# Half 0's convolution split in two: two channel tiles before the recurrence's inverse, two after it

## The chip, the cores and the metric

One core of one Trainium2 chip runs the whole program in one launch. The metric is device time in microseconds (us); the time shown for a kernel is the median of its runs. The profile is of one further execution, and its time is given beside its span.

## The reference

One layer of a hybrid decoder over 1024 tokens of width 1024, with 256 memory tokens, all in float32. The input projection of the normed x has two uses: its first 1024 columns feed a causal convolution group of 512 channels, the others a recurrent (RWKV-7) group of 8 heads. What the change touches is this much of it:

```
h = rms_norm(x, g[0])
p = h @ w_in_first
y_conv = conformer_conv(p[..., :2 * D_CONV], ...)   # u * sigmoid(u'), 31 taps per channel, layer norm, silu
y_rwkv = rwkv7_mix(p[..., 2 * D_CONV:], ...)        # token-shift mix, gates, recurrence, group norm
x = x + rms_norm(concat(y_conv, y_rwkv) @ w_out, g[1])
mem_n = rms_norm(mem, mem_norm_g)
x = x + rms_norm(cross_attention(rms_norm(x, g[2]), mem_n, wq, wkv, wo), g[3])
x = x + rms_norm(swiglu(rms_norm(x, g[4]), w_gu, w_down), g[5])
```

## The kernel before

**Halves and phases.** The 1024 tokens are worked in two halves of TB = 512. For each half the kernel projects (`w_in_block`), prepares the recurrence's factors (`rwkv_prep`), inverts small triangular blocks (`rwkv_values`, `rwkv_inverse`), runs the recurrence over eight chunks of 64 tokens (`rwkv_chain`, whose results leave in `rwkv_out`), runs the convolution (`conv`), and then the output projection, cross-attention and feed-forward. Results of one phase go to DRAM tiles (pdr for mixer features, hd for the convolution's input, yd for the mixer's output) and are loaded from there by the next.

**Matmuls.** Every weight panel is split on chip in a high part (ScalarE, line 170) and a low part (VectorE, line 171), and each product is three matmuls (lines 193 to 195). One input panel of 128 features over 512 tokens is 24 matmuls of 512 columns. `wload` takes the raw panel in a ring of four tiles and the two parts in rings of two. All DMAs but a few go through SyncE's queue.

**The projection's columns.** `conv_cols` = (4, 0, 6, 2) and `mix_cols` = (20, 12, 8, 16, 14, 10, 18) name pairs of panels. Panel 20 carries the low-rank inputs, 12 and 14 the first and second two key tiles, 8 and 10 the receptance, 16 and 18 the values. A mixer panel is evacuated at lines 305 to 312, a convolution panel at lines 321 and 325. `rwkv_prep` is a generator: its first part works on head pairs 0 and 1 and needs the first keys; its second part begins with `norms(1)`, which needs both tiles of block 14. The last vector operation of a head pair is the gate product at line 549.

**The convolution.** Each of four channel tiles loads one row block `hin` from hd, starts its accumulator on ScalarE (line 348) and adds 30 taps on VectorE (line 350). When all four are done, `conv_norm` takes two sums over channels by matmul (lines 365 and 378), a reciprocal square root, and stores each tile to yd (line 392). The accumulators are one tile of four parts. The bias tile `cb` is one buffer that half 1's convolution takes over.

**The order.** The program is traced as one list, and a planner orders each engine's instructions from that list: an instruction that stands earlier goes first when its inputs and its tile are there. `weave` mixes two generators by the us that they say they cost; `fill` draws panels of half 1 into gaps of the output phases by the amounts in `self.fl`. The memory maps (`memory_maps`, lines 823 to 856) fold the attention's weights with the normed memory, four heads of them. Pools stand on two stacks, left and right, and a pool pushed after another was popped stands on its addresses and waits for its tiles one by one.

In before, half 0 goes: norm x and the memory; block 20; blocks 12, 8, 16; the preparation's first part; blocks 14, 10, 18; its second part; values, inverse; convolution panels; recurrence; and a weave of (two heads of maps, norm of half 1's x, two heads of maps, half 1's convolution panels, three of its mixer blocks) with the convolution of half 0. The last four mixer blocks are the filler of what follows. The pool conv0 stands on the left where the preparation and the inverse were.

Of the kernel before, what the change touches and what calls it, by code (L numbers as in the profile page):

```python
# [9 lines left out]
F32 = mybir.dt.float32  # L10
# [7 lines left out]
P = 128  # L18
# [3 lines left out]
TB = 512  # L22
NB = SEQ // TB
MEM = 256
DR = 512
# [36 lines left out]
def drain(*gens):  # L62
    for g in gens:
        for _ in g:
            pass


class Trunk:
# [259 lines left out]


    def conv(self, b, pool):  # L330
        acc = pool.tile([P, 4, TB], F32, tag="acc", name="acc")
        yield from self.conv_taps(b, pool, acc)
        yield from self.conv_norm(b, pool, acc)

    def conv_taps(self, b, pool, acc):
        nc = self.nc

        if b == 1:
            self.cb = self.cp.tile([P, 8], F32, tag="convb", name="convb")
            nc.scalar.copy(out=self.cb[:, 0:4], in_=self.col("conv_b"))  # L340
            nc.scalar.copy(out=self.cb[:, 4:8], in_=self.lbh)
        t0 = b * TB
        for j in range(4):
            h = pool.tile([P, 576], F32, tag="hin", bufs=2, name="hin")[:, 0:TB + CONVW - 1]
            nc.sync.dma_start(out=h, in_=self.hd[j * P:(j + 1) * P, t0:t0 + TB + CONVW - 1])
            a = acc[:, j, :]
            w = lambda k: self.cwh[:, j * CONVW + k:j * CONVW + k + 1]
            nc.scalar.activation(out=a, in_=h[:, 0:TB], func=AF.Identity, scale=w(0), bias=self.cb[:, j:j + 1])  # L348
            for k in range(1, CONVW):
                nc.vector.scalar_tensor_tensor(out=a, in0=h[:, k:k + TB], scalar=w(k), in1=a,  # L350
                                               op0=ALU.mult, op1=ALU.add)
                if k % 6 == 0:
                    yield 4.0

    def conv_norm(self, b, pool, acc):
# [2 lines left out]
        tmp = lambda name: pool.tile([P, TB], F32, tag="t", bufs=2, name=name)  # L358
        add = lambda out, x, y: nc.vector.tensor_tensor(out=out, in0=x, in1=y, op=ALU.add)
        sa, sb = tmp("lnsa"), tmp("lnsb")  # L360
        add(sa, acc[:, 0, :], acc[:, 1, :])
        add(sb, acc[:, 2, :], acc[:, 3, :])
        add(sa, sa, sb)
        ps = self.pn.tile([P, TB], F32, tag="n", name="psln")
        nc.tensor.matmul(ps, self.ones, sa, start=True, stop=True)
        for j in range(4):
            nc.vector.scalar_tensor_tensor(out=acc[:, j, :], in0=ps, scalar=-1.0 / DR, in1=acc[:, j, :],
                                           op0=ALU.mult, op1=ALU.add)
        yield 6.0
        sa = tmp("lnsq")  # L370
        nc.scalar.activation(out=sa, in_=acc[:, 0, :], func=AF.Square)
        for j in range(1, 4):
            sb = tmp("lnsq")
            nc.scalar.activation(out=sb, in_=acc[:, j, :], func=AF.Square)
            add(sb, sa, sb)
            sa = sb
        ps = self.pn.tile([P, TB], F32, tag="n", name="psln2")
# [4 lines left out]
        self.rsqrt(ry, rs, pool.tile([P, TB], F32, tag="t", bufs=2, name="lnt"))  # L382
        yield 6.0
        for j in range(4):
            a = acc[:, j, :]
            nc.vector.tensor_tensor(out=a, in0=a, in1=ry, op=ALU.mult)
            th = pool.tile([P, TB], F32, tag="t", bufs=2, name="lnth")
            sc, bi = self.lgh[:, j:j + 1], self.cb[:, 4 + j:5 + j]
            nc.scalar.activation(out=th, in_=a, func=AF.Tanh, scale=sc, bias=bi)
            nc.scalar.activation(out=a, in_=a, func=AF.Identity, scale=sc, bias=bi)  # L390
            nc.vector.scalar_tensor_tensor(out=a, in0=th, scalar=1.0, in1=a, op0=ALU.add, op1=ALU.mult)
            nc.sync.dma_start(out=self.yd[j * P:(j + 1) * P, t0:t0 + TB], in_=a)
            yield 2.0
# [550 lines left out]
    def run(self):  # L944
# [4 lines left out]
        def push(name, side):  # L949
            opened[name] = tc.tile_pool(name=name, bufs=1, side=side, reuse_waits="tile")  # L950
            return opened[name].__enter__()
# [3 lines left out]
                opened.pop(n).__exit__(None, None, None)  # L955


        self.fl = dict(res0=6.0, load0=6.0, soft0=5.0, res1=5.0, load1=16.0, soft1=0.0)
        self.filler = None
        self.credit = 0.0  # L960
        conv_cols, mix_cols = (4, 0, 6, 2), (20, 12, 8, 16, 14, 10, 18)
# [3 lines left out]

        a1 = push("a1", R)
        ev = push("ev", R)
        mk = push("mk", R)
        a0 = push("a0", R)
        h0, h1, mT = self.pairs(a0), self.pairs(a1), self.pairs(mk, MEM, "m")  # L970
        self.xn = 4
        self.xp = push("xa", L)
        self.normed(self.x, 0, (0, 4), h0, "g_mix", 2)
        drain(self.w_in_block(0, h0, ev, mix_cols[:1], 2))
        self.normed(self.mem, 0, (0, 2), mT, "g_mem", 2)
        pop("xa")
        self.lora_split(ev)
        self.nc.scalar.dma_start(out=self.hd[:, 0:CONVW - 1].rearrange("(j p) t -> p j t", p=P), in_=self.state[:, :, 0:CONVW - 1])
# [1 line left out]
        pp = push("prep0", L)  # L980
        prep = self.rwkv_prep(0, pp)
        next(prep)
        drain(self.w_in_block(0, h0, ev, mix_cols[4:]))
        drain(prep)
        pop("prep0")

        tp = push("tt0", L)
        TT = tp.tile([P, NCH * HP, CH], F32, tag="TT", name="TT")
        pp = push("inv0", L)
        self.rwkv_values(0, pp)  # L990
        self.rwkv_inverse(0, pp, TT)
        drain(self.w_in_block(0, h0, ev, conv_cols))
        pop("inv0", "a0")
        kv = push("kv", R)
        self.xn = 2
        self.xp = push("xb", R)
        kp = push("conv0", L)

        gp = push("gn0", L)
        mp = push("mix0", L)  # L1000
# [4 lines left out]
                yield 1.0 * 2  # L1005
        maps = self.memory_maps(mT, ev, kv)
        w1 = self.w_in_block(1, h1, ev, conv_cols)
        w1m = self.w_in_block(1, h1, ev, mix_cols[:3])
        main = chain(islice(maps, 16), next_norm(), maps, w1, w1m)
        drain(weave(main, self.conv(0, kp), 1.0))  # L1010
        pop("mix0", "gn0", "conv0", "tt0", "xb", "kv", "mk")
        self.filler = self.w_in_block(1, h1, ev, mix_cols[3:])

        yp = push("y0", L)
        a2 = push("a2", L)
# [106 lines left out]
```

## Time and profile before

| what | value |
|---|---|
| median of 3 runs | 1640.81 us (1639.69 to 1641.62) |
| profiled execution | 1639.56 us, span 1637.8 us |
| TensorE matmul busy | 1521.8 us (93%) |
| TensorE weight loads busy | 1240.5 us (76%) |
| VectorE busy | 1066.9 us (65%) |
| ScalarE busy | 685.9 us (42%) |
| mean granted TensorE clock | 0.967 |

Busy time is the time in which an engine executes; shares are of the span. Times in rows are us from the span's start. The matmuls' ends are modelled, so the spacing of their starts tells more than their length. L350 is line 350 of the kernel; PE is TensorE, PEld its weight loads, DVE VectorE, ACT ScalarE, SPq SyncE's queue.

### The profile page before, as it was taken

To read this page: it belongs to the slowest core of one execution; us is meant where nothing else is said; L and a number is where in the kernel's file an instruction comes from. 1 tells how busy PE (TensorE), PEld (TensorE's weight loads), DVE (VectorE), ACT (ScalarE), POOL (GpSimd) and SP (SyncE) were. 2 spreads that over 40 slices of the span, in tenths; PEclk is the share of its full clock that TensorE was granted. 3 is DMA by queue.
4 is the path that set the end of the run, shared out by engine and by line. 5 is a ranking of instruction groups with operands and counts; after the bars stand their busy time and mean duration, and the time that the engine had idled before them with its cause. 6 is when DMAs were issued, how large, how long until landed. Compare 5 with 4: busy or idle time off the path is not lost.

```text
span 1637.8 us, 22612 instructions
## 1 busy us (share of the span) xinstructions
PE 1521.8 (93%) x8688; PEld 1240.5 (76%) x8688; DVE 1066.9 (65%) x1704; ACT 685.9 (42%) x1064; POOL 54.6 (3%) x102
## 2 busy tenths in 40 slices
PE   7999878999659789699999999999999999999997
PEld 6787767877447577577788777888887888888886
DVE  5687675999879996686775455637537634344445
ACT  5645355544343336456323344524435332222222
POOL 1000100000000100100000000001001100000000
PEclk9999988999879899899999999999999999999999
DMA  6576995774344423545885444445236633333331
GB/s 201 176 230 183 297 339 153 258 234 142 103 141 158 143 86 93 190 124 150 234 248 139 143 145 138 149 124 200 87 97 225 231 98 95 101 92 101 92 90 52
DMA packets 175643, 257.36 MB, mean 157 GB/s; under 512 B 68912, under 2 KB 110000, under 8 KB 175536
## 3 DMA queue, kind: packets, MB, share of 16 engines
q1 hardware_dynamic: 174576, 255.08, 50.0%
q8 instruction: 68, 1.11, 0.3%
q10 hardware_dynamic: 960, 0.85, 0.2%
q14 instruction: 39, 0.32, 0.1%
HBM read 196.58 MB, written 59.31 MB: 156 GB/s over the span
## 4 chain that ended last, share of the span: by engine, by line
PE 85%; DVE 5%; DMA 4%; ACT 4%; issue 1%; SPq 0%; POOL 0%; DVEq 0%; POOLq 0%; ACTq 0%
PE psf L193 15%; PE psf L195 15%; PE psf L194 15%; PE pst L193 10%; PE pst L194 10%; PE pst L195 10%; PE psg L522 2%; DVE acc L350 1%; PE pstr L273 1%; PE pspr L436 1%; DVE wlo L171 1%; ACT whi L170 1%; DMA xt<-in_x_dram 1%; DVE ya L762 1%; PE psq L684 1%
## 5 line engine op out<-in xcount | busy, mean ns | idle before, releaser
L170 ACT CAST whi<-wraw 128x1024 fp32r<-128x1024 f32 x256 | 268.4, 1050 | 567.3 <-PE psf L194 228.6
L171 DVE TENSOR_TENSOR wlo<-wraw,whi 128x1024 fp32r<-128x1024 f32 x256 | 312.5, 1222 | 278.2 <-ACT whi L170 277.1
L193 PE MATMUL psf<-ahi,whi 128*128 128x512 f32 (+1 forms) x1200 | 458.7, 384 | 6.9 <-ACT whi L170 3.5
L195 PE MATMUL psf<-ahi,wlo 128*128 128x512 f32 (+1 forms) x1200 | 456.1, 381 | 1.8 <-DVE wlo L171 1.7
L194 PE MATMUL psf<-alo,whi 128*128 128x512 f32 (+1 forms) x1200 | 457.8, 382 | 0.0
L193 PEld LDWEIGHTS psf<-ahi,whi 128*128 128x128 f32 x1200 | 228.8, 191 | 53.1 <-ACT whi L170 6.0
L195 PEld LDWEIGHTS psf<-ahi,wlo 128*128 128x128 f32 x1200 | 228.4, 190 | 45.7 <-DVE wlo L171 3.8
L194 PEld LDWEIGHTS psf<-alo,whi 128*128 128x128 f32 x1200 | 229.4, 191 | 42.4 <-issue 1.0
L350 DVE SCALAR_TENSOR_TENSOR acc<-hin,cols,acc 128x512 f32<-128x512 f32 x240 | 170.7, 743 | 5.2 <-ACT acc L348 4.9
L193 PE MATMUL pst<-whi,ahi 128*128 128x512 f32 x384 | 138.9, 400 | 21.9 <-ACT ahi L170 17.1
L194 PE MATMUL pst<-wlo,ahi 128*128 128x512 f32 x384 | 152.0, 398 | 1.4 <-DVE wlo L171 1.4
L195 PE MATMUL pst<-whi,alo 128*128 128x512 f32 x384 | 146.6, 391 | 0.0
L194 PE MATMUL pst<-wlo,fhi 128*128 128x512 f32 x352 | 137.4, 391 | 0.0
L193 PE MATMUL pst<-whi,fhi 128*128 128x512 f32 x352 | 134.2, 392 | 0.0
L195 PE MATMUL pst<-whi,flo 128*128 128x512 f32 x352 | 134.0, 390 | 0.0
L193 PEld LDWEIGHTS pst<-whi,ahi 128*128 128x128 f32 x384 | 72.9, 191 | 40.2 <-ACT ahi L170 18.6
L929 DVE SCALAR_TENSOR_TENSOR ftg<-ftg,psf 128x512 f32<-128x512 f32 x44 | 30.2, 686 | 86.1 <-PE psf L195 86.0
L194 PEld LDWEIGHTS pst<-wlo,ahi 128*128 128x128 f32 x384 | 73.3, 191 | 17.0 <-DVE wlo L171 1.8
L195 PEld LDWEIGHTS pst<-whi,alo 128*128 128x128 f32 x384 | 71.8, 188 | 15.1 <-issue 0.5
L233 POOL TENSOR_TENSOR rstd<-rstd,mhalf 128x1 f32<-128x1 f32 x50 | 37.2, 753 | 1319.0 <-DVE rstd L232 1319.0
L911 DVE TENSOR_TENSOR ya<-pst,ya 128x512 f32<-128x512 f32 x80 | 54.0, 687 | 40.6 <-PE pst L195 40.3
L194 PEld LDWEIGHTS pst<-wlo,fhi 128*128 128x128 f32 x352 | 66.1, 188 | 14.0 <-DVE wlo L171 0.4
(240 smaller groups left out, 1690.2 us busy)
## 6 DMA issues: line engine op xcount, KB each, us to landing
wraw<-in_w_gu_dram SPq DMA_DIRECT2D x88, 512.0 KB, 3.7
wraw<-in_w_in_dram SPq DMA_DIRECT2D x44, 512.0 KB, 4.2
wraw<-in_w_down_dram SPq DMA_DIRECT2D x44, 512.0 KB, 3.6
wraw<-in_wkv_dram SPq DMA_DIRECT2D x16, 512.0 KB, 5.2
am<-amd SPq DMA_DIRECT2D x16, 512.0 KB, 4.8
wraw<-in_w_out_dram SPq DMA_DIRECT2D x16, 512.0 KB, 3.7
wraw<-gd SPq DMA_DIRECT2D x16, 512.0 KB, 4.5
wraw<-vwd SPq DMA_DIRECT2D x16, 512.0 KB, 3.4
```

Source lines behind the costliest of these rows:

```text
L170: self.nc.scalar.copy(out=hi, in_=src)
L171: self.nc.vector.tensor_tensor(out=lo, in0=src, in1=hi.bitcast(F32), op=ALU.subtract)
L193: mm(ps, w[0], x[0], start=start, stop=False)
L194: mm(ps, w[0], x[1], start=False, stop=False)
L195: mm(ps, w[1], x[0], start=False, stop=stop)
L233: nc.gpsimd.tensor_tensor(r, r, self.mhalf, op=ALU.pow)
L273: nc.tensor.transpose(ps[:, t * P:(t + 1) * P], xt[:, k * P:(k + 1) * P], self.ident)
L350: nc.vector.scalar_tensor_tensor(out=a, in0=h[:, k:k + TB], scalar=w(k), in1=a, op0=ALU.mult, op1=ALU.add)
L436: nc.tensor.matmul(ps, w, x, start=i == 0, stop=i == len(terms) - 1)
L522: nc.tensor.matmul(pg[g][:, i, :], bk[half[g], c + i, :], aq[half[g], :, c + i, :], start=True, stop=True)
L911: nc.vector.tensor_tensor(out=y, in0=ps, in1=y, op=ALU.add)
L929: nc.vector.scalar_tensor_tensor(out=tg, in0=tg, scalar=0.5, in1=pu, op0=ALU.mult, op1=ALU.mult)
```

## The change

The accumulators become four tiles of their own, and `conv_taps` takes the channel tiles that it is to do and a pool for them. The pool conv0 moves to the right stack, below a0, and is open from the start. In half 0 the convolution panels are traced ahead of blocks 14, 10 and 18. The taps of tiles 0 and 1 are traced right behind the preparation, before the inverse; those of tiles 2 and 3, in a small pool conv0b, and the layer norm are woven with what follows the inverse. The memory's norm and its pairs (mk, with the row pool xb) move from the start to behind the preparation, onto the left stack, where the preparation's tiles stood, and use another PSUM ring. The weave's main line now is: norm of half 1's x, four heads of maps, half 1's convolution panels, one mixer block instead of three. Six blocks instead of four are left as filler, and `res0`, the amount drawn at each of half 0's residual tiles, goes from 6 to 8.

```diff
     def conv(self, b, pool):
-        acc = pool.tile([P, 4, TB], F32, tag="acc", name="acc")
-        yield from self.conv_taps(b, pool, acc)
+        acc = []
+        yield from self.conv_taps(b, pool, pool, acc, range(4))
         yield from self.conv_norm(b, pool, acc)
 
-    def conv_taps(self, b, pool, acc):
+    def conv_taps(self, b, pool, apool, acc, cols):
         nc = self.nc
 
-        if b == 1:
+        if b == 1 and not acc:
             self.cb = self.cp.tile([P, 8], F32, tag="convb", name="convb")
...
-        for j in range(4):
+        for j in cols:
             h = pool.tile([P, 576], F32, tag="hin", bufs=2, name="hin")[:, 0:TB + CONVW - 1]
             nc.sync.dma_start(out=h, in_=self.hd[j * P:(j + 1) * P, t0:t0 + TB + CONVW - 1])
-            a = acc[:, j, :]
+            a = apool.tile([P, TB], F32, tag="acc%d" % j, name="acc")
+            acc.append(a)
...
-        self.fl = dict(res0=6.0, load0=6.0, soft0=5.0, res1=5.0, load1=16.0, soft1=0.0)
+        self.fl = dict(res0=8.0, load0=6.0, soft0=5.0, res1=5.0, load1=16.0, soft1=0.0)
...
         a1 = push("a1", R)
         ev = push("ev", R)
-        mk = push("mk", R)
+        kp = push("conv0", R)
         a0 = push("a0", R)
-        h0, h1, mT = self.pairs(a0), self.pairs(a1), self.pairs(mk, MEM, "m")
+        h0, h1 = self.pairs(a0), self.pairs(a1)
         self.xn = 4
         self.xp = push("xa", L)
         self.normed(self.x, 0, (0, 4), h0, "g_mix", 2)
         drain(self.w_in_block(0, h0, ev, mix_cols[:1], 2))
-        self.normed(self.mem, 0, (0, 2), mT, "g_mem", 2)
         pop("xa")
...
         next(prep)
+        drain(self.w_in_block(0, h0, ev, conv_cols))
         drain(self.w_in_block(0, h0, ev, mix_cols[4:]))
         drain(prep)
         pop("prep0")
 
+        acc = []
+        drain(self.conv_taps(0, kp, kp, acc, range(2)))
+        self.xn = 2
+        self.xp = push("xb", L)
+        mk = push("mk", L)
+        mT = self.pairs(mk, MEM, "m")
+        self.normed(self.mem, 0, (0, 2), mT, "g_mem", 2, (self.pd, "d"))
         tp = push("tt0", L)
         TT = tp.tile([P, NCH * HP, CH], F32, tag="TT", name="TT")
         pp = push("inv0", L)
         self.rwkv_values(0, pp)
         self.rwkv_inverse(0, pp, TT)
-        drain(self.w_in_block(0, h0, ev, conv_cols))
         pop("inv0", "a0")
         kv = push("kv", R)
-        self.xn = 2
-        self.xp = push("xb", R)
-        kp = push("conv0", L)
+        ka = push("conv0b", L)
...
         w1 = self.w_in_block(1, h1, ev, conv_cols)
-        w1m = self.w_in_block(1, h1, ev, mix_cols[:3])
-        main = chain(islice(maps, 16), next_norm(), maps, w1, w1m)
-        drain(weave(main, self.conv(0, kp), 1.0))
-        pop("mix0", "gn0", "conv0", "tt0", "xb", "kv", "mk")
-        self.filler = self.w_in_block(1, h1, ev, mix_cols[3:])
+        def conv_rest():
+            yield from self.conv_taps(0, kp, ka, acc, range(2, 4))
+            yield from self.conv_norm(0, kp, acc)
+        w1m = self.w_in_block(1, h1, ev, mix_cols[:1])
+        main = chain(next_norm(), maps, w1, w1m)
+        drain(weave(main, conv_rest(), 1.0))
+        pop("mix0", "gn0", "conv0b", "tt0", "mk", "xb", "kv", "conv0")
+        self.filler = self.w_in_block(1, h1, ev, mix_cols[1:])
```

In `conv_norm` only `acc[:, j, :]` becomes `acc[j]`.

## Rows read from the trace of the kernel before

**Rows 1.** The page: busy time of the engines; the costliest group of taps.
```profile
PE 1521.8 (93%) x8688; PEld 1240.5 (76%) x8688; DVE 1066.9 (65%) x1704; ACT 685.9 (42%) x1064; POOL 54.6 (3%) x102
...
L350 DVE SCALAR_TENSOR_TENSOR acc<-hin,cols,acc 128x512 f32<-128x512 f32 x240 | 170.7, 743 | 5.2 <-ACT acc L348 4.9
```

**Rows 2.** Windows by stage: start:end, length, busy time (count) by engine, clock, DMA.
```profile
111.00:173.00 62.00, 62.00 (x344) 48.42 (x342) 45.81 (x65) 30.38 (x41) 0.86 (x4) 1.00 0.73 224
200.00:258.00 58.00, 39.02 (x237) 34.29 (x238) 41.22 (x95) 28.05 (x47) 1.10 (x2) 0.79 0.90 288
258.00:430.50 172.50, 168.16 (x1602) 140.49 (x1601) 151.53 (x240) 90.89 (x140) 0.00 (x0) 1.00 0.61 194
430.50:468.40 37.90, 4.56 (x7) 1.05 (x5) 26.17 (x43) 16.92 (x25) 0.00 (x0) 0.55 0.29 90
468.40:516.70 48.30, 45.74 (x192) 37.04 (x193) 45.10 (x70) 15.84 (x28) 0.55 (x1) 0.97 0.45 142
516.70:553.30 36.60, 24.50 (x110) 19.54 (x109) 36.25 (x62) 14.85 (x23) 7.00 (x7) 0.86 0.74 245
657.00:690.00 33.00, 20.50 (x89) 15.91 (x88) 22.51 (x36) 17.70 (x33) 4.66 (x9) 0.79 0.67 216
```

**Rows 3.** Chain of waits, 404 to 470: start, length, what.
```profile
439.71 0.70 DVE lnsb L359
...
461.22 2.00 DMA yd<-acc
```

**Rows 4.** Timeline of SyncE's queue, 460 to 470: start, length of issue.
```profile
460.52 1.02 SPq L392 DMA_DIRECT2D yd<-acc  x2
463.27 0.37 SPq L741 DMA_DIRECT2D araw<-yd  x1
```

**Rows 5.** Timeline of TensorE, 430 to 470; idle time before in brackets.
```profile
430.48 0.39 PE L195 MATMUL psf<-ahi,wlo 128*128 128x512 f32 x1
...
468.35 0.80 PE L193 MATMUL pst<-whi,ahi 128*128 128x512 f32 x1 [17.08 <-ACT ahi L170]
```

**Rows 6.** Source lines, half 0: count, ns min/median/max, first to last start.
```profile
L307 DVE SCALAR_TENSOR_TENSOR evq<-psf,cols,evq x14: 735/744/750, 33.5 to 111.2; 128x511 f32<-128x511 f32 x14
...
L325 DVE SCALAR_TENSOR_TENSOR evh<-tg,psf x4: 677/678/681, 132.7 to 171.7; 128x512 f32<-128x512 f32 x4
...
L468 DVE TENSOR_SCALAR rn<-psbk x2: 681/686/692, 119.4 to 120.0; 128x512 f32<-128x512 f32 x2
...
L549 DVE SCALAR_TENSOR_TENSOR v<-v,cols,pspr x4: 739/743/747, 113.1 to 180.7; 128x512 f32<-128x512 f32 x4
...
L679 PE MATMUL psp<-uv,am x128: 222/222/271, 265.4 to 392.6; 128*64 128x64 f32 x128
...
L733 SPq DMA_DIRECT2D yd<-Y x4: 370/371/376, 331.7 to 438.2; - x4
```

**Rows 7.** VectorE alone in two windows.
```profile
100.00:181.00 81.00, 59.75 (x89) 1.00 0.78 234
...
900.00:1034.00 134.00, 70.65 (x108) 1.00 0.46 142
```

**Rows 8.** Window of four panels' matmuls alone (tile psf).
```profile
516.70:538.60 21.90, 21.77 (x95) 17.76 (x96) 2.50 (x5) 2.04 (x3) 1.00 0.79 260
```

**Rows 9.** Timeline of VectorE, 86.5 to 88.
```profile
87.07 0.74 DVE L307 SCALAR_TENSOR_TENSOR evq<-psf,cols,evq 128x511 f32<-128x511 f32 x1
```

**Rows 10.** The same source lines in half 1.
```profile
L549 DVE SCALAR_TENSOR_TENSOR v<-v,cols,pspr x4: 740/744/748, 747.9 to 820.2; 128x512 f32<-128x512 f32 x4
...
L679 PE MATMUL psp<-uv,am x128: 222/222/270, 900.1 to 1023.1; 128*64 128x64 f32 x128
...
L733 SPq DMA_DIRECT2D yd<-Y x4: 359/374/378, 957.7 to 1054.2; - x4
```

**Rows 11.** The memory rows' load on SyncE; the last memory pair on VectorE.
```profile
19.52 0.80 SPq L289 DMA_DIRECT2D xt<-in_mem_dram  x2
...
49.99 0.48 DVE L277 SCALAR_TENSOR_TENSOR alo<-pstr,cols,ahi 128x256 fp32r<-128x256 f32 x1
```

More of the change, by code (lines that the diff above doesn't have):

```diff
@@ L360, in conv_norm @@
         sa, sb = tmp("lnsa"), tmp("lnsb")
-        add(sa, acc[:, 0, :], acc[:, 1, :])
-        add(sb, acc[:, 2, :], acc[:, 3, :])
+        add(sa, acc[0], acc[1])
+        add(sb, acc[2], acc[3])
         add(sa, sa, sb)
@@ L366, in conv_norm @@
         for j in range(4):
-            nc.vector.scalar_tensor_tensor(out=acc[:, j, :], in0=ps, scalar=-1.0 / DR, in1=acc[:, j, :],
+            nc.vector.scalar_tensor_tensor(out=acc[j], in0=ps, scalar=-1.0 / DR, in1=acc[j],
                                            op0=ALU.mult, op1=ALU.add)
@@ L370, in conv_norm @@
         sa = tmp("lnsq")
-        nc.scalar.activation(out=sa, in_=acc[:, 0, :], func=AF.Square)
+        nc.scalar.activation(out=sa, in_=acc[0], func=AF.Square)
         for j in range(1, 4):
             sb = tmp("lnsq")
-            nc.scalar.activation(out=sb, in_=acc[:, j, :], func=AF.Square)
+            nc.scalar.activation(out=sb, in_=acc[j], func=AF.Square)
             add(sb, sa, sb)
@@ L384, in conv_norm @@
         for j in range(4):
-            a = acc[:, j, :]
+            a = acc[j]
             nc.vector.tensor_tensor(out=a, in0=a, in1=ry, op=ALU.mult)
```

## Prediction

> **What bounds the kernel now.** I read the page first, then the windows stage by stage, then the chain of waits, then the timelines around each gap. The page gives TensorE 93% busy and VectorE 65% [rows 1]: matmuls bound most of the span, and a change that takes no matmul away can win only where TensorE stands still. The windows show where that is [rows 2]. From 430.5 to 468.4 TensorE works 4.6 of 37.9 us, by far the widest hole. The chain of waits crosses it on the convolution's own steps [rows 3]: the last taps end, the layer norm begins at 439.71, its four stores go out from 461.22, the row load for the output projection is issued at 463.27 [rows 4], and the first w_out matmul runs at 468.35, 37.5 us after the last projection's start at 430.48 [rows 5]. VectorE is what holds it up: it is busy 151.5 of 172.5 us in the stage before [rows 2], and 120 taps of 0.71 us (170.7 us over 240 [rows 1]), 85 us, are the largest part of that. The recurrence is no excuse for that hole: its last output store is issued at 438.2 [rows 6], 22 us before the first of the convolution's. Smaller holes: 200 to 258 (39.0 busy of 58.0, granted clock 0.79), 516.7 to 553.3 (12.1 idle) and 657 to 690 (12.5 idle) [rows 2]. From 111 to 173 TensorE is full [rows 2].
>
> **The change part by part.** All matmuls, taps and transfers stay; what changes is order and place, so the sum is one of dates.
>
> *Taps of tiles 0 and 1 leave the late stage.* 60 of 120 taps, 60 x 0.71 = 43 us of VectorE, move ahead of the inverse. Their cover is VectorE's idle time beside the preparation: 81.0 - 59.75 = 21 us between 100 and 181 [rows 7], plus what the later second half of the preparation leaves free. I take all but some 8 of the 60 as hidden, and the rest as 5 us on the inverse below. Their two row loads join SyncE's queue behind the stores of the convolution panels; weights are four buffers ahead there, so I cost them at nothing; with that lead gone a load costs TensorE a few us once. Splitting acc in four tiles adds no instruction.
>
> *The convolution's panels go ahead of three mixer blocks.* A panel of 24 matmuls takes 21.9/4 = 5.5 us [rows 8], so eight take 43.8. The second key block then comes 43.8 later: its last evacuation, at 87.07 in before [rows 9], falls at about 131. The preparation's second half starts from it. In before its norm's clamp is at 119.4 and its last gate product at 180.7 [rows 6], 61 us with the convolution's panels in TensorE's queue throughout. Bounds for the shift of that last product: 43.8 if nothing is recovered; 12 if the 32 us that lay between key and clamp, and the queueing behind panels that now are done, are mostly recovered. I take 23, between the two and nearer to the lower, since panels end about 155 (111.2 [rows 6] plus eight) and TensorE then has little else: last product at 204.
>
> *The inverse.* From that product to the recurrence's first matmul: 265.4 - 180.7 = 84.7 [rows 6]; in half 1, which has the same steps, 900.1 - 820.2 = 79.9 [rows 10]. I take 84.7 plus 5 for spilled taps and the memory norm's vector work, 90; bounds 80 and 105 (30 taps spilled). The recurrence starts at 294, not 265.
>
> *The recurrence.* From its first matmul to its last output store: 438.2 - 265.4 = 172.8 with 120 taps on VectorE [rows 6], 1054.2 - 900.1 = 154.1 in half 1 without any [rows 10], where VectorE is busy 70.65 of 134 us [rows 7]. With 60 taps I take 158, near the second; bounds 154 and 173. Last store: 204 + 90 + 158 = 452, 14 later than before. The convolution has then long been finished (43 us of taps and 29 us from layer norm to first w_out matmul, 468.35 - 439.71 [rows 3, 5], begun before 300), so this store now releases w_out.
>
> *w_out.* Store to row load took 463.27 - 460.52 = 2.8 [rows 4], load to first matmul 468.35 - 463.27 = 5.1 [rows 4, 5]. So the recurrence's rows are multiplied from 452 + 7.9 = 460. A quarter of w_out (the convolution's rows, first column half) can be done by then; three quarters are six panels' worth, 6 x 5.5 = 33. w_out ends at 493 against 516.7 (the window's end [rows 2]): 24 us earlier.
>
> *Panels moved behind.* w1m shrinks from three blocks to one: four panels, 21.9 us [rows 8], leave the stage before w_out and become filler, where res0 = 8 puts two more in each of the two residual gaps. Those gaps have 12.1 + 12.5 = 24.6 us idle [rows 2]. I take 3 us as not fitting; bounds 0 and 21.9.
>
> *The memory norm* moves from the start to behind prep0's tiles, on a side where its rows and pairs stand on prep0's old addresses. In before the memory rows' load is at 19.52 and the last pair at 49.99 [rows 11], beside a full TensorE. Now its cover is gone: weight tiles are filled in the program's order, so no later panel can pass the memory maps, and TensorE idles from the panels' end at about 155 until the first pairs exist, but for the second half's products. Some of prep0's buffers come free before its last product, so I put the first map at 207, three us after it, against 173 in before (right behind the last panel's evacuation at 171.7 [rows 6]). That is 34 us later; I take 12 off, for the preparation's matmuls and the idle time that the same stretch of before has (19 us idle from 200 to 258 [rows 2]): 22 us of matmuls behind. It is about what the four panels moved away give back: the last projection before w_out stays near 431, and hides behind the recurrence.
>
> Sum: 24 - 3 = 21 us. The profiled execution took 1639.56 (span 1637.8 and 1.8 around it); 1618.6. The median of the runs shown, 1640.81, is 1.25 above it, so 1619.
>
> **Rivals.**
>
> *B, TensorE is the bound.* The preparation recovers more, the recurrence's store comes at 435 or earlier, and w_out follows the projections at 431 without a wait: end at 431 + 43.6 = 475, 42 earlier, less 3: 1602. For it: half 1's bare times. Against it: the second key block really is eight panels later.
>
> *C, no change.* None of the 43.8 is recovered: last product 224, last store 224 + 90 + 158 = 472, w_out ends at 513, 4 us won, 3 of them lost on fillers: 1640. For it: the page has TensorE as the busiest engine, and no matmul goes away. The Trainium skill, Perfetto Trace Analysis, Identifying the Most-Contended Engine, says that improving a kernel is in general improving its most-contended engine, and judges TensorE by its weight loads' share, here 76% [rows 1], the highest on the page; by that rule this change, which relieves VectorE, gives nothing: 1641. The trace does not bear it out between 430.5 and 468.4, where TensorE works 4.6 of 37.9 us [rows 2].
>
> *D, slower: the memory norm is late.* Its place is the stretch between the panels' end and the first map. It waits for prep0's last buffers, then needs up to the 30 us that before shows from load to last pair [rows 11]. Each us after 207 moves the projections' end. It decides the time from about 225 on (the convolution's quarter of w_out, 11 us, then no longer fits before 460), and the kernel is slower than before from about 246 (w_out at 431 + 39, end at 514, and the 3). At 260 it is 1655. For it: the tiles' place. Against it: the 30 us were spent beside full engines, the bare steps are short.
>
> *E, the change doesn't do what it says.* The taps of tiles 0 and 1 find no room beside the preparation and run in front of the inverse: 43 us instead of 5, last store 490, w_out ends at 531: 1658. For it: VectorE is 74% busy there already. Against it: the preparation's second half is gone from the stretch in which the taps become ready.
>
> **How the numbers follow.** Forecast 0.48, B 0.18, C 0.14, D 0.12, E 0.08. C lies on the edge: 0.04 of it faster, 0.10 unchanged. Faster by over 0.2% (3.3 us, about what a measurement of this kernel tells from nothing): 0.70; within: 0.10; slower: 0.20. The forecast's own range is 1606 to 1630, from the shift of 12 to 30 and the recurrence's 154 to 165. To leave out no more than 2 in 10, the range reaches from B's 1602 to 1647, past C and into D.
>
> **What would show it.** Right: the last gate product of half 0 near 204, the recurrence's first matmul near 294 and last store near 452, the convolution's stores some 30 us before that, the hole before w_out shorter than 20 us, an idle stretch of TensorE between 155 and 207, and the holes at the two residuals closed. Wrong: the product after 220 (C), taps still running when the inverse starts (E), the first memory map after 225 (D), or w_out starting straight behind a projection (B). The largest doubt is the 23 us of the second half's delay; every us there is one of the end.

## The result, and the profile after

The changed kernel takes 1628.19 us (median of 5 runs, 1627.84 to 1634.64) against 1640.81 (1638.97 to 1643.81) for the kernel before in the same session: a ratio of 0.9933, 95% interval 0.9911 to 0.9956. The profiled execution took 1627.87 us with a span of 1626.2, 11.7 less than that of before. The page answers to [rows 1]:

```profile
PE 1529.1 (94%) x8688; PEld 1250.7 (77%) x8688; DVE 1065.9 (66%) x1704; ACT 683.3 (42%) x1062; POOL 56.7 (3%) x102
```

The same work is done; TensorE stands still less. The windows show where (start:end, length, busy time and count of TensorE's matmuls, its weight loads, VectorE, ScalarE and GpSimd, then granted clock and DMA):

```profile
111.00:155.00 44.00, 43.99 (x192) 35.48 (x190) 41.43 (x66) 17.15 (x22) 0.11 (x1) 1.00 0.51 161
155.00:201.00 46.00, 29.69 (x165) 23.88 (x164) 42.13 (x66) 17.27 (x25) 2.62 (x5) 0.55 0.66 194
201.00:260.00 59.00, 24.95 (x121) 18.54 (x120) 41.26 (x114) 21.34 (x41) 6.79 (x11) 0.60 0.63 183
...
430.00:470.00 40.00, 37.81 (x163) 30.02 (x163) 40.00 (x65) 14.51 (x22) 0.00 (x0) 1.00 0.64 204
...
520.00:560.00 40.00, 33.51 (x155) 27.17 (x154) 39.61 (x69) 14.26 (x20) 5.97 (x5) 0.91 0.49 160
...
660.00:690.00 30.00, 25.80 (x119) 19.88 (x117) 18.79 (x31) 17.40 (x26) 1.68 (x4) 0.94 0.52 162
```

The hole ahead of w_out is gone: TensorE works 37.8 of 40 us from 430, where it worked 4.6 of 37.9 [rows 2]. The holes at the two residuals have shrunk: the idle time of TensorE between w_out's first matmul and 720 fell from 33.4 to 14.2 us. But a new sparse stretch stands between 155 and 260, with 54.6 of 105 us busy and a granted clock near 0.6, where before TensorE was full to 173 and two thirds busy from 200 to 258 [rows 2]. The dates of half 0's steps, by source line (duration, first and last start; the lines moved by one from 347 on, so L550 and L680 are the L549 and L679 of [rows 6]):

```profile
L351 DVE SCALAR_TENSOR_TENSOR acc<-hin,cols,acc x60: 725/743/755, 98.9 to 190.1; 128x512 f32<-128x512 f32 x60
...
L550 DVE SCALAR_TENSOR_TENSOR v<-v,cols,pspr x4: 740/744/748, 110.0 to 201.5; 128x512 f32<-128x512 f32 x4
...
L277 DVE SCALAR_TENSOR_TENSOR alo<-pstr,cols,ahi x24: 470/474/483, 216.7 to 253.3; 128x256 fp32r<-128x256 f32 x24
...
L824 ACT CAST kvh<-psf x16: 364/367/374, 257.4 to 369.7; 128x256 fp32r<-128x256 f32 x16
...
L680 PE MATMUL psp<-uv,am x128: 222/222/271, 279.0 to 398.4; 128*64 128x64 f32 x128
...
L734 SPq DMA_DIRECT2D yd<-Y x4: 370/380/385, 351.8 to 440.6; - x4
```

All 60 early taps start by 190.1, before the last gate product at 201.5. The recurrence runs from 279.0 to its last store at 440.6. The first map's evacuation comes at 257.4; in before it came at 178.4. TensorE's timeline shows what stands ahead of the maps (idle time before an instruction in brackets), then what stands ahead of w_out:

```profile
212.95 2.08 PE L577 MATMUL psv<-ident,v 128*128 128x128 f32 x8 [11.62 <-DMA v<-pdr]
...
226.54 1.09 PE L577 MATMUL psv<-ident,v 128*128 128x128 f32 x4 [6.91 <-DMA v<-pdr]
...
234.42 1.09 PE L273 MATMUL pstr<-ident,xt 128*128 128x128 f32 x4 [5.49 <-DVE xt L259]
...
246.67 1.09 PE L273 MATMUL pstr<-ident,xt 128*128 128x128 f32 x4 [6.20 <-DVE xt L259]
...
460.25 0.39 PE L194 MATMUL psf<-alo,whi 128*128 128x512 f32 x1
460.48 0.39 PE L195 MATMUL psf<-ahi,wlo 128*128 128x512 f32 x1
460.70 0.39 PE L193 MATMUL pst<-whi,ahi 128*128 128x512 f32 x1
```

Between 230 and 253 the transposes of x rows (xt) are half 1's norm, which the change traces ahead of all maps. And w_out (pst) starts at 460.70 straight behind a projection (psf), with no wait: neither the convolution nor the recurrence, whose rows were stored at 440.6, releases it now. w_out's last matmul ends at 505.1 instead of 516.9, and what follows takes 1121.0 us as before (1120.9). So the whole gain is 11.8 us at w_out, and in this kernel six filler blocks instead of four cost next to nothing. That is not so in most of the runs below: with the same six blocks, what follows w_out takes 1125.6 to 1130.1 us in all but one of them, and none shows why.

### The profile page after: what moved, and what is told of

It is laid out like the page before. It is cut to its first block, busy times and chain, and to the rows that moved or that the text cites. A ratio compares the mean times of both kernels' runs of the same rounds, so it can differ in the third digit from the quotient of the medians.

```text
span 1626.2 us, 22610 instructions
## 1 busy us (share of the span) xinstructions
PE 1529.1 (94%) x8688; PEld 1250.7 (77%) x8688; DVE 1065.9 (66%) x1704; ACT 683.3 (42%) x1062; POOL 56.7 (3%) x102
## 4 chain that ended last, share of the span: by engine, by line
PE 60%; DVE 1%; ACT 1%; issue 0%; POOL 0%; POOLq 0%; DVEq 0%; ACTq 0%
PE psf L193 10%; PE psf L195 10%; PE psf L194 10%; PE pst L194 8%; PE pst L193 8%; PE pst L195 8%; PE psg L523 1%; PE pstr L273 0%; DVE ya L763 0%; PE pspr L437 0%; PE psp L680 0%; PE pss L695 0%; PE psu L690 0%; PE psq L685 0%; DVE wlo L171 0%
## 5 line engine op out<-in xcount | busy, mean ns | idle before, releaser
L195 PEld LDWEIGHTS pst<-whi,alo 128*128 128x128 f32 x384 | 71.7, 188 | 14.5
```

Source lines behind the costliest of these rows:

```text
L195: mm(ps, w[1], x[0], start=False, stop=stop)
```

## The experiments

Theory 1: after the change TensorE's queue up to w_out is the bound, because the maps come late. Rivals: VectorE is the bound (theory 2); the late memory norm, not the order of the maps, is what the change pays for (theory 3). The dates below are starts from each profile, in us: the last gate product of half 0; how many of the convolution's taps start between it and the recurrence's first matmul; the length of that stretch, called the inverse here; the recurrence's last store; w_out's first matmul and the end of its last; the length of what is left of the span behind that end; and the median.

```
kernel                          product  taps  inverse  store  w_out        behind  median
before                           180.7     0     84.7   438.2  468.4-516.9  1120.9  1639 to 1641
changed                          201.5     0     77.5   440.6  460.7-505.1  1121.0  1628.2
new split alone                  180.6     0     81.7   427.3  457.3-503.6  1127.1  1633.7
old split                        203.4     0     77.0   443.8  485.7-530.4  1122.8  1651.5
maps first                       201.5     0     99.3   468.5  460.5-516.9  1129.8  1646.5
mixers first                     196.5    20     91.9   457.8  456.2-506.4  1128.0  1639.2
panels split                     194.4     0     77.6   437.2  451.9-497.4  1125.6  1625.3
taps behind, pool early          201.2     0     78.5   441.2  462.2-506.3  1121.0  1630.5
taps behind, pool late           209.3    23     95.7   471.5  466.4-520.3  1130.1  1653.5
taps in the inverse              181.7    60    137.1   463.6  455.7-512.4  1127.3  1641.2
same, memory late                154.1    60    132.6   444.8  456.0-503.8  1127.1  1629.6
memory late alone                154.4     7     75.8   383.3  448.8-495.1  1128.7  1624.7
same, half 1's norm first        154.3     4     76.8   384.5  450.0-496.9  1126.6  1625.3
memory late, half of the panels  168.9    60    124.8   457.3  448.8-506.1  1127.1  1634.9
```

**The two halves of the change.** The new split of half 1's mixer blocks in the kernel before, and the old split in the changed one:

```diff
-        self.fl = dict(res0=6.0, load0=6.0, soft0=5.0, res1=5.0, load1=16.0, soft1=0.0)
+        self.fl = dict(res0=8.0, load0=6.0, soft0=5.0, res1=5.0, load1=16.0, soft1=0.0)
...
-        w1m = self.w_in_block(1, h1, ev, mix_cols[:3])
+        w1m = self.w_in_block(1, h1, ev, mix_cols[:1])
...
-        self.filler = self.w_in_block(1, h1, ev, mix_cols[3:])
+        self.filler = self.w_in_block(1, h1, ev, mix_cols[1:])
```

> One edit to the kernel before: only the new split (one mixer block of half 1 ahead of w_out, six as filler, res0 = 8), nothing of the convolution moved. Theory 1 (in the kernel before the convolution, not TensorE, releases w_out, so panels taken away from before it only widen the hole, but they fill the two residual gaps): those gaps shrink by 10 to 20 us: 1621 to 1631, so most of the change's gain could have been had by this alone. Rival (the fillers do not fit, or the gain needs the convolution moved): 1637 to 1644.

> One edit to the changed kernel: the split of half 1's mixer blocks goes back to that of the kernel before, three ahead of w_out and four as filler, res0 = 6. Theory 1 (TensorE is the bound ahead of w_out): the four panels, 21.9 us, stand in front of w_out again and the two residual gaps open again: about 20 slower, 1648. Rival (the four panels hide beside the recurrence and only the residual gaps of 12 us tell): 1632 to 1640.

Measured: 1633.7 for the split alone (ratio 0.9963, 0.9950 to 0.9976), a little above the range of theory 1; 1651.5 for all but the split (1.0068, 1.0050 to 1.0085), where theory 1 had said 1648. Alone, the split wins 6 us and everything else loses 12; together they win 12.6. TensorE's timelines say why, first that of before with the new split, then that of the change with the old one:

```profile
430.19 2.08 PE L365 MATMUL psln<-lnsa,ones 128*128 128x512 f32 x2 [17.80 <-DVE lnsa L359]
...
457.30 0.80 PE L193 MATMUL pst<-whi,ahi 128*128 128x512 f32 x1 [17.02 <-ACT ahi L170]
```

```profile
485.48 0.39 PE L195 MATMUL psf<-ahi,wlo 128*128 128x512 f32 x1
485.70 0.61 PE L193 MATMUL pst<-whi,ahi 128*128 128x512 f32 x2
```

In the first the convolution still releases w_out, and its norm comes 11 us earlier (430.2 instead of 441.2), since VectorE has four panels less to split and evacuate ahead of it (its busy time from 258 to the norm is 154.1 us instead of 162.1); what the expectation had called a mere widening of the hole was a gain. w_out ends 13.3 us earlier (503.6), and the fillers cost 6.2 of that behind it. In the second TensorE goes from projection to w_out without a wait, 25 us later than in the changed kernel: with the convolution out of the way each panel ahead of w_out costs its time in full. The four panels bring work for VectorE too, so this run alone does not set theory 1 against theory 2; the changed kernel's own window from the first map's evacuation to w_out does:

```profile
257.00:460.70 203.70, 195.15 (x1841) 168.33 (x1840) 168.46 (x257) 125.84 (x199) 0.00 (x0) 0.98 0.73 237
```

TensorE works 195.2 of 203.7 us there, and waits 2.1 us for a low part from VectorE. So TensorE's queue bounds the changed kernel from the first map up to w_out, as theory 1 says, and VectorE (theory 2), busy all of 430 to 470, does not.

**The order of the maps.**

```diff
-        main = chain(next_norm(), maps, w1, w1m)
+        main = chain(islice(maps, 16), next_norm(), maps, w1, w1m)
```

> One edit to the changed kernel: sixteen steps of the memory maps are traced ahead of half 1's norm again, as in the kernel before. Theory 1 (after the change TensorE's own queue is the bound up to w_out, because the first map waits behind half 1's norm): the first map matmul comes at about 222 us instead of 252, the idle stretches of 30 us between 201 and 247 mostly go, w_out starts behind the recurrence's last store (440.6 + 7.9 = 448.5) instead of at 460.5, so about 12 us are won: about 1616. Theory 2 (VectorE, busy for 40.0 of 40 us before w_out, is the bound): no gain, 1628 within 3.

Measured: 1646.5 (1.0040, 1.0027 to 1.0053), 18 us slower than the changed kernel. Its source lines, TensorE's timeline, and the window of the inverse, first in the changed kernel and then in this run:

```profile
L824 ACT CAST kvh<-psf x16: 357/365/373, 224.8 to 353.4; 128x256 fp32r<-128x256 f32 x16
...
L680 PE MATMUL psp<-uv,am x128: 222/222/368, 300.8 to 429.9; 128*64 128x64 f32 x128
...
L734 SPq DMA_DIRECT2D yd<-Y x4: 370/370/385, 371.2 to 468.5; - x4
...
287.44 1.09 PE L273 MATMUL pstr<-ident,xt 128*128 128x128 f32 x4 [9.32 <-DVE rstd L232]
...
460.52 0.79 PE L193 MATMUL pst<-whi,ahi 128*128 128x512 f32 x1 [6.55 <-ACT ahi L170]
...
472.43 2.08 PE L195 MATMUL pst<-whi,alo 128*128 128x512 f32 x4 [8.16 <-DVE alo L171]
...
201.50:279.00 77.50, 42.47 (x466) 35.53 (x466) 47.99 (x121) 32.32 (x58) 6.29 (x11) 0.67 0.68 196
...
201.50:300.80 99.30, 70.38 (x661) 62.50 (x661) 61.74 (x135) 49.93 (x84) 5.92 (x10) 0.79 0.81 250
```

The maps came when theory 1 said (224.8), and yet it lost: the recurrence starts 21.8 us later (300.8), its last store is 27.9 later (468.5), and w_out, begun at 460.52, stands for 8.16 us for the low parts of its rows, which VectorE makes only behind the recurrence's last operations; the recurrence's own rows land at 474.2. Two heads of maps and half 1's norm now both fall between the last gate product and the recurrence, and stretch that from 77.5 to 99.3. The inverse's longest part is a chain of small steps on VectorE (lines 612 and 613 of the changed kernel, 31 steps each). From its first step to the end of its last it takes 40.2 us in the changed kernel (217.1 to 257.3) and 54.6 here (217.0 to 271.6). VectorE's work in the whole stretch grows from 48.0 to 61.7 us, and 12.2 of these 13.8 us are the low parts of weights (line 171, 16 instead of 6). The other 7.5 us of the stretch come behind the chain, where TensorE stands 9.32 us in front of half 1's transposes, whose norm isn't ready. So the idle TensorE of 201 to 253 is not lost time to be filled: work for TensorE brings work for VectorE, and that lengthens the inverse. The second half of theory 1, that the late maps cost the end, falls: maps that came 33 us earlier brought the end of the projections forward by 7 (the last one starts at 453.6 instead of 460.5). Of the 20.5 us between the two profiles 11.8 are there at w_out's end, and the others come behind it.

**The order of half 0's panels.** All convolution panels behind the mixer blocks, or only those of tiles 2 and 3:

```diff
-        drain(self.w_in_block(0, h0, ev, conv_cols))
         drain(self.w_in_block(0, h0, ev, mix_cols[4:]))
+        drain(self.w_in_block(0, h0, ev, conv_cols))
```

```diff
-        drain(self.w_in_block(0, h0, ev, conv_cols))
+        drain(self.w_in_block(0, h0, ev, conv_cols[:2]))
         drain(self.w_in_block(0, h0, ev, mix_cols[4:]))
+        drain(self.w_in_block(0, h0, ev, conv_cols[2:]))
```

> One edit to the changed kernel: the three mixer blocks go ahead of the convolution's panels again, so the second key block is evacuated near 87 instead of 131. Theory 1 (the late second half of the preparation holds back prep0's tiles, and with them the memory norm, the maps and the projections): the last gate product comes some 20 us earlier (near 181), everything to w_out's start moves by 10 to 20: 1608 to 1618. Rival (the taps of tiles 0 and 1 then start only at the panels' end near 155 and run in front of the inverse, 43 us of VectorE): the inverse ends where it did or later, 1625 to 1640.

> One edit to the changed kernel: only the convolution's panels of tiles 0 and 1 go ahead of the three mixer blocks, those of tiles 2 and 3 behind them. The second key block comes 22 us earlier (its last evacuation near 114 instead of 136). If the preparation's second half waits for it, the last gate product comes 10 to 15 earlier and everything to w_out too: 1615 to 1620. Rival (the taps of tiles 0 and 1, which VectorE must do in the same stretch, hold the preparation and the inverse up instead): 1626 to 1636.

Measured: 1639.2 (0.9996, 0.9985 to 1.0008), the rival's form; and 1625.3 (0.9907, 0.9884 to 0.9931), between the two expectations. With all panels behind, the last product comes 5 us earlier, but 20 taps fall in the inverse, which takes 14.4 longer. With half of them behind, no tap does, the product comes 7.1 earlier (194.4), and w_out 8.8 earlier (451.9). Of the 43.8 us by which the panels put the second key block back, the last product feels 21, and 22 us given back there are worth 7.

**The place of the taps.** First the taps of tiles 0 and 1 moved in the text to behind the inverse, their pool open from the start as in the change; then that pool opened behind the inverse as well:

```diff
-        drain(self.conv_taps(0, kp, kp, acc, range(2)))
...
         def conv_rest():
+            yield from self.conv_taps(0, kp, kp, acc, range(2))
             yield from self.conv_taps(0, kp, ka, acc, range(2, 4))
```

```diff
-        kp = push("conv0", R)
...
         kv = push("kv", R)
+        kp = push("conv0", R)
         ka = push("conv0b", L)
```

> One edit to the changed kernel: the taps of tiles 0 and 1 go behind the inverse, so that all four tiles run beside the recurrence. If TensorE's queue alone decides (projections to 460.5), the 60 taps cost little: 1628 to 1633. If VectorE decides, the convolution's stores go from 414 to about 450 and w_out starts behind them: 1640 to 1650.

> One edit to the changed kernel: the convolution's pool is opened only after the inverse's has closed, so that the taps of tiles 0 and 1 can't start before (where only their place in the text moved, they still ran from 98 to 185). All else stays as in the changed kernel. If TensorE's projections (to 460.9) set w_out's start, the convolution may end 43 us later (its norm from 381 to about 424, w_out's row load some 25 behind) at no cost: 1626 to 1632. If the early taps carry the gain, VectorE, 111 of 130 us busy from 300 to 430, is overfull and w_out starts at 470 or later: 1638 to 1646.

Measured: 1630.5 (0.9944, 0.9929 to 0.9960) and 1653.5 (1.0083, 1.0067 to 1.0100). The first did not do what it says: the 60 taps still ran from 95.6 to 189.3, because rows and tiles were there and VectorE had room. It tells only that two builds of one order stand 2 us apart. The second moved them, though not as far as expected (they begin at 156.2):

```profile
L351 DVE SCALAR_TENSOR_TENSOR acc<-hin,cols,acc x120: 724/745/753, 156.2 to 389.8; 128x512 f32<-128x512 f32 x120
...
L550 DVE SCALAR_TENSOR_TENSOR v<-v,cols,pspr x4: 739/742/746, 105.3 to 209.3; 128x512 f32<-128x512 f32 x4
...
L680 PE MATMUL psp<-uv,am x128: 222/222/271, 305.0 to 422.6; 128*64 128x64 f32 x128
...
L734 SPq DMA_DIRECT2D yd<-Y x4: 370/380/553, 370.6 to 471.5; - x4
```

23 of them fall in the inverse; the recurrence starts at 305.0 and its last store is 31 us later than in the changed kernel, five us behind w_out's first matmul. The cost up to w_out's end, 15.2 us, comes through the inverse and not through the convolution, whose norm starts 18 us later (398.7) and is still early; 9.1 more come behind w_out. So within the changed kernel the early taps have to be done before the inverse, not merely before the recurrence. The next pair puts all 60 inside the inverse: memory norm, panels and maps in the order of the kernel before, with the new split, conv0 opened behind the preparation, and

```diff
         self.rwkv_inverse(0, pp, TT)
         drain(self.w_in_block(0, h0, ev, conv_cols))
+        drain(self.conv_taps(0, kp, kp, acc, range(2)))
```

and the same with the memory norm where the change has it; in that run conv0 is also where the change has it, on the right and open from the start, so the two differ in more than the memory norm.

> The changed kernel with the memory norm at the start, the convolution's panels behind the mixer blocks and two heads of maps ahead of half 1's norm, all as in the kernel before; only the taps of tiles 0 and 1 stay early (their tiles on the left side, traced behind the inverse, so that they fill VectorE's gaps beside it), and the new split stays. Theory 3 (the late memory norm, not the taps, is what the change pays for): the convolution of the run with the new split alone (w_out's first matmul at 457.3 behind 45 us of idle TensorE) ends up to 43 us earlier, the recurrence's last store at about 440 releases w_out at 446 to 449: 1622 to 1626. Rival (taps beside the inverse push the recurrence back by as much): 1630 to 1640.

> The same kernel with one more part of the change, the memory norm behind the preparation's tiles. Theory 3: the first map moves from about 175 to 222 or later, TensorE loses some 29 us of work before 300, and the projections end that much later: 15 to 25 slower than the run with the memory norm at the start. Rival (the idle time is only moved, since the hole before w_out takes it up): within 5 of it.

Measured: 1641.2 (1.0008, 0.9993 to 1.0023) and 1629.6 (0.9938, 0.9916 to 0.9959). Both expectations of theory 3 failed, and the first run came a little above its rival's range. The windows of the inverse, with the split alone and with the taps in it:

```profile
180.60:262.30 81.70, 62.50 (x630) 55.19 (x630) 55.35 (x120) 41.77 (x68) 2.59 (x6) 0.85 0.86 262
...
181.70:318.80 137.10, 106.41 (x926) 94.95 (x925) 112.10 (x202) 66.35 (x102) 4.78 (x7) 0.88 0.79 243
```

60 taps in the inverse make it 137 us, 55 more than with the split alone. VectorE's work in it grows by 56.8 us (55.35 to 112.10): 43.4 of taps and 17.2 more of low parts of weights, which the longer stretch took in (neighbours overlap a little in the records). Its idle time hardly moves (26.4 and 25.0 us), so almost none of the new work fell into it. And the run with the late memory norm was 12 us faster, not slower: its last gate product comes at 154.1 instead of 181.7. Theory 3 falls for these kernels; no run moves the memory norm of the changed kernel itself back to the start. The next run takes that part by itself.

**The memory norm.** The kernel before with the new split, and of the change only this (conv0 opens on the right, where there is room now):

```diff
         drain(self.w_in_block(0, h0, ev, mix_cols[:1], 2))
-        self.normed(self.mem, 0, (0, 2), mT, "g_mem", 2)
...
         pop("prep0")
+        self.xn = 2
+        self.xp = push("xb", L)
+        mk = push("mk", L)
+        mT = self.pairs(mk, MEM, "m")
+        self.normed(self.mem, 0, (0, 2), mT, "g_mem", 2, (self.pd, "d"))
```

then with `next_norm()` ahead of all maps, as in the change.

> The kernel before with the new split (1633.7 by itself) and one more part of the change, the memory norm behind the preparation's tiles; panels, taps and maps in the order of the kernel before. If the late memory load holds the convolution's panels back and leaves TensorE to the preparation, as in the run with late memory norm and taps beside the inverse (last gate product 154), the recurrence starts near 240 and its last store falls before 420; w_out is then set by the convolution's norm or by the projections near 450: 1618 to 1628. Rival (the maps and panels that come later cost TensorE what the preparation wins, and without early taps the convolution ends at 457 or later): 1633 to 1645.

> The same with half 1's norm ahead of all maps, as in the changed kernel. If maps ahead of the inverse's matmuls hold the recurrence back (22 us in the run that put two heads of maps first again), this one starts its recurrence earlier by 10 to 20 and is 5 to 15 faster than the same without it. Rival (order of norm and maps tells only beside early taps): within 4.

Measured: 1624.7 (0.9904, 0.9887 to 0.9920) and 1625.3 (0.9908, 0.9893 to 0.9924): within the range of the first expectation, and the order of norm and maps is worth nothing here. With no panel and no tap moved in the text this is as fast as the whole change, by the medians 3.5 us faster; the intervals overlap. w_out ends 10.0 us earlier than in the changed kernel (495.1), but what follows takes 7.7 longer. Timelines of SyncE, VectorE and TensorE, a window and two source lines of the first:

```profile
108.37 1.00 SPq L177 DMA_DIRECT2D wraw<-in_w_in_dram  x1
...
157.39 3.58 SPq L289 DMA_DIRECT2D xt<-in_mem_dram  x2
...
181.04 0.33 SPq L177 DMA_DIRECT2D wraw<-in_w_in_dram  x1
...
107.13 1.22 DVE L171 TENSOR_TENSOR wlo<-wraw,whi 128x1024 fp32r<-128x1024 f32 x1
...
170.70 1.57 PE L273 MATMUL pstr<-ident,xt 128*128 128x128 f32 x6 [0.40 <-DVE alo L277]
171.97 0.80 PE L193 MATMUL psf<-ahi,whi 128*128 128x512 f32 x1
...
111.00:155.00 44.00, 35.45 (x169) 27.61 (x168) 33.38 (x50) 18.61 (x26) 3.12 (x7) 0.51 0.66 195
...
L679 PE MATMUL psp<-uv,am x128: 222/222/370, 230.2 to 341.9; 128*64 128x64 f32 x128
...
L733 SPq DMA_DIRECT2D yd<-Y x4: 370/374/378, 297.9 to 383.3; - x4
```

Between 108.4 and 181.0 no weight panel is loaded, but the queue is not what stops them: SyncE goes on issuing the preparation's transfers all that time. By 108.4 two of the convolution's panels have been split (the second's low part at 107.13), which fills the rings of two, and the loads of four more are issued, which fills the ring of raw panels. Still the first of their matmuls runs at 171.97, right behind the last transposes of the memory pairs. The late memory norm takes its PSUM tiles from the projections' ring (`self.pd`), and the convolution's panels are traced behind it, so their tiles come after its own. That fits the dates; that the ring is the cause is not shown, since no run gives the memory norm another one. In the meantime the preparation has TensorE to itself, its last product comes at 154.4, and the recurrence starts at 230 and is done at 383, 57 us ahead of the changed kernel's. The convolution runs earlier beside it (its norm starts at 401.4, with the split alone at 430.2), so w_out again starts behind a projection (448.8). The panels lose less by their delay than the recurrence and the convolution gain. The last run gave that stretch half of its panels back:

```diff
         drain(self.w_in_block(0, h0, ev, mix_cols[4:]))
+        drain(self.w_in_block(0, h0, ev, conv_cols[:2]))
...
-        drain(self.w_in_block(0, h0, ev, conv_cols))
+        drain(self.w_in_block(0, h0, ev, conv_cols[2:]))
```

> The kernel with the new split and the late memory norm alone (1624.7), with one edit: the convolution's panels of tiles 0 and 1 go ahead of the memory norm in the order of the weights, right behind the mixer blocks; those of tiles 2 and 3 stay behind it. In that run no weight load is issued from 108.4 to 181.0 and TensorE, at a granted clock of 0.51, is busy 35.5 of 44 us with the preparation alone, while its projections (to 449.0) set w_out's start and the recurrence's last store (383.3) is 65 us early. If TensorE's queue is what decides, four panels (22 us) in that stretch bring w_out forward by 8 to 15, though the preparation ends later: 1610 to 1618. Rival (each panel there delays the preparation by as much as it takes): 1622 to 1628.

Measured: 1634.9 (0.9965, 0.9954 to 0.9977), outside both. The panels cost the preparation 14.5 us (168.9), but the loss came behind it: the rows of tiles 0 and 1 were ready from 215, their taps went into the inverse (all 60), and that took 124.8 instead of 75.8. w_out began at 448.8, stood for 7.0 us until 461 for low parts that VectorE made behind the recurrence's last operations, and went on when the recurrence's rows landed at 463.0.

## Why the prediction was right, and where it was not

The sign and the first half of the mechanism were right: the hole of [rows 2] came from the convolution on VectorE, taps fit beside the preparation, and the hole closed. What was to release w_out then was not right: the forecast had the recurrence's last store, and the run shows the last projection. The size was 9 us too large, and that it was not further off is partly luck: the recurrence came 11 us earlier than forecast and the projections 30 later. Step by step, forecast and measured:

- *Last gate product*: 204, measured 201.5. None of the 60 early taps spilled behind it, where 8 had been allowed for.
- *Inverse*: 90, measured 77.5. The forecast took before's 84.7 and added taps and the memory norm; it missed that the maps, which before stood in this stretch, leave it, and with them the low parts of their weights on VectorE. Maps first again made it 99.3.
- *Recurrence*: 158, measured 161.6 with 78 taps beside it (60 of half 0, 18 of half 1). But the number of taps is not what sets it: with 102 taps beside it, it took 153.1 in the run with the late memory norm alone (230.2 to 383.3).
- *Its last store*: 452, measured 440.6, 11 early by the inverse. By the prediction's 7.9 us from store to matmul it would have released w_out at 440.6 + 7.9 = 448.5, an estimate.
- *First memory map and last projection*: 207 and "near 431"; measured 252.2 and 460.5. **This is the term that was mis-sized.** The memory pairs were done at 221, not 207, since the rows' load is issued at 204.9, behind the preparation's last store; and half 1's norm, which the change traces ahead of the maps, was not in the sum at all: its transposes run until 252.5, and the first map behind them. The four panels that move behind w_out gave back less than the late maps took. How much of the 30 us the maps' date costs stays open: in the run with maps first it was 33 us better and the projections' end only 7.
- *w_out*: end at 493, measured 505.1, 12 us later, because it follows the projections. *Fillers*: 3 us of cost, measured 0.1 (1121.0 against 1120.9). Together they are the 9 us: 12.1 - 2.9 = 9.2. That the fillers were free is luck too: with the split alone they cost 6.2.

Of the rivals, B's form came true (w_out straight behind a projection) but at 460.7 and not at 431. D's condition came true, first map after 225, and its price did not: it would have made the kernel slower from 246 on, but the map came at 252 and the kernel was faster, because the end of the projections does not follow the first map us for us: 431 + 45 would be 476, and it came at 460.5. E did not happen, but its mechanism is among the most expensive ones here: runs with 20 to 60 taps in the inverse are 5 to 25 us slower than their nearest run without (mixers first and taps behind against the change, taps in the inverse against the new split alone, the same with memory late and half of the panels against the late memory norm alone). In C, the rule of the Trainium skill (Perfetto Trace Analysis, Identifying the Most-Contended Engine), to optimize the most-contended engine first, was weighed with the shares of the whole span, by which the change gives nothing. It does not fit before, where the hole was VectorE's and the change won 12.6 us; it fits the changed kernel up to w_out, where four panels more for TensorE cost 25 us.

Also wrong in the reasons, though not in the sum: that the memory norm's late place is a pure cost (by itself, with conv0 on the right, it won 9 us over the split alone), and a reading: the 37.5 us between the last projection and w_out run from that projection's end, from its start they are 37.9. The forecast also did not see that the split frees VectorE ahead of the convolution, worth 11 us of the norm's date.

What stays open: how two heads of maps and half 1's norm would each stretch the inverse without the other; what holds the convolution's panels back behind the late memory norm; why what follows w_out takes 5 to 9 us longer in most runs with the new split than in the changed kernel; and whether the version with the late memory norm alone is truly faster than the change.

## What to carry to other kernels

The idle time of an engine beside a long dependent chain is not free room when the chain itself runs on that engine: 60 taps, some 43 us of VectorE, put into the inverse lengthened it by 49 to 57 us together with the weights' low parts that came with them, while VectorE's idle time there stayed at 20 to 26 us. Beside the preparation the same taps showed no such cost (last product 201.5 with all 60 there, 209.3 when they began at 156). When a hole is closed, look up what stands next in line by date (here projections at 461, recurrence at 449, convolution long done), and size the fillers for that one: the split of half 1's blocks was worth 6 us while VectorE was the bound and 23 once TensorE was. Moving a step moves what is traced behind it and shares its tiles, which here was worth as much as the move that was meant.

## What the runs showed of the hardware that was not expected

With the late memory norm alone TensorE worked on no panel from 106 on, and the granted clock over 111 to 155 was 0.51, the lower of its two levels (1.2 GHz), with 35.5 of 44 us busy. In before it was 1.00 there, and TensorE was full [rows 2]. Yet the rest of the preparation, from the end of the last mixer panel's evacuation to the last gate product, took 154.4 - 109.7 = 44.7 us at the lower clock and 180.7 - 112.0 = 68.7 at the higher. So the convolution's and the maps' panels beside it, on TensorE and on VectorE, cost this chain more than a halved clock did. In the changed kernel the inverse ran at a granted clock of 0.60 (201 to 260) and was 7 us shorter than in before, at about 0.8 [rows 2]; its longest part is VectorE's.
